# Branch a's operands, spilled rows and branch b's loads asked for at other steps

## The chip, the cores and the metric

The kernel runs on one core of one Trainium2 chip. The metric is the device time of one execution in microseconds. The kernel before took 1357.1 us, the median of 3 runs (1355.99 to 1358.39). Engines are named as in the profile: PE multiplies matrices, PEld loads its weights, DVE (vector), ACT (scalar) and POOL (GpSimd) work on tiles, SP issues most DMAs; POOL issues others on a queue of its own.

## The reference

One layer of an encoder on 1024 tokens of width 1024, in float32: a mixer of two branches merged by gates, then a SwiGLU network, each between two RMS norms. The mixer, cut to what the change touches:

```python
def mixer(h, w_in, b_f, conv_w, w_branch, w_out):
    proj = jnp.einsum("bsd,dn->bsn", h, w_in)
    q, k, v, f_logit, g_b, g_c, hc, gate_conv, gate_attn = jnp.split(proj, _SPLITS, axis=-1)
    ya = g_b * causal_depthwise_conv(g_c * hc, conv_w)
    ...
    yb = forgetting_attention(q.reshape(shp), k.reshape(shp), v.reshape(shp), logf)
    yb = yb.reshape(bsz, s_len, ATTN_WIDTH)
    ya_d = jnp.einsum("bsc,cd->bsd", ya, w_branch[0])
    yb_d = jnp.einsum("bsc,cd->bsd", yb, w_branch[1])
    merged = jax.nn.sigmoid(gate_conv) * ya_d + jax.nn.sigmoid(gate_attn) * yb_d
    return jnp.einsum("bsd,de->bse", merged, w_out)
```

Below, branch a is the convolution's (`ya`, `w_branch[0]`, `gate_conv`), branch b the attention's (`yb`, `w_branch[1]`, `gate_attn`).

## The kernel before, in words

Every float32 product is made of three matmuls on high and low halves (`split`, `mm3`): ACT copies the high half, DVE subtracts it for the low one. Most products use Strassen's scheme in Winograd's form: seven products of quarters (B11, B21, B22, T1 to T4 on the tokens' side; A11, A12, A22, S1 to S4 on the weights'). All instructions are recorded on line 76, so tile names tell them apart.

**Stages.** Up to 55 us the first norm and v; then the projections in 18 pairs of 128 columns (`jobs`, `strassen`, line 681; a pair is 84 matmuls on PE); from about 410 us attention in 21 steps (`steps`, line 1145; the loop adds two closing steps, t = 21 and 22), with branch a's products between them; from 551 us their end, from 588 branch b's eight 128-column products for each half of the tokens (`pbb`), then w_out, and the SwiGLU network from 632 us on.

**Side work of the projections.** Generators run a step at a time between the products of a pair (`plans`). `wa_steps` (line 762) makes branch a's weight operands: rows k and k+2 of `w_branch[0]` are loaded into `rows4`, four sums are formed there in two more quarters, everything is split and spilled to `wa_dram`; then `load_rows` (line 813) asks for the next pair of rows. The parts take turns in the tiles `r0`, `l0`, `h0`. `ya_steps` (line 819) does the same to the tokens of branch a, into `ya_ops`. A scheduler sets the order here, except for the instructions that are made while `strict` names their engine.

**Branch a within attention** (order written by hand: `strict[0] = engines`, line 1352). Its operands come back from memory. `load_y` (line 1363) loads a token operand (1 MB) into one of the four places h0, h1, l0, l1, by the table `HOME` (line 1360); `load_w` a weight operand (256 KB) into a ring of five small tiles (`s4`, two `s4h`, two `s4l`), in the order of use (`w_order`, `next_w`); `load_sg` a gate, in a ring of four. 28 chunks of six matmuls, P1 to P7 for each of four p (256 output columns each), are dealt to steps 2 to 22 (`chunks`, line 1510); the last six follow as `A_TAIL` (line 1519). P6 needs T1, P7 needs B22. A chunk's `drain` takes its PSUM bank into `um` on DVE, and P7 of a p goes into the bank of its P6. What is loaded at the end of step t stands in `at[t]` (lines 1569 to 1580). SP issues these DMAs one by one; one that waits holds up all behind it. In the same queue stand the reciprocals of the softmax sums (`inverse_rows`, line 1450): DVE copies `rT`, SP writes it (`ri_dram`), and reads it back as a broadcast (`rb`), twice at the end, for each half of the last head pair.

**Branch b.** `split_wb` splits its four blocks of weights (`raw`, then `wbh`, `wbl`) at steps 17, 19, 21, 22. In its loop (line 1791) the gate of each product is loaded, and in the first four passes a block of `w_out` (`load_wo`, line 1719); `strict` is empty there, so that the scheduler may issue them earlier.

## Time and profile before

| what | us |
|---|---|
| median of 3 runs | 1357.1 |
| profiled execution, its own time | 1352.99 |
| its span (first to last instruction) | 1351.2 |
| PE busy | 1309.4 |
| end of attention and branch a, 551 to 589: PE busy | 24.18 of 38 |
| branch b's products, 589 to 632: PE busy | 43.0 of 43 |
| projections, 300 to 396: PE busy | 78.8 of 96 |

In a row of the timeline come the start, the duration, the engine, line and operation, out<-in by the program's names, how many in a row, and in brackets how long the engine stood idle before it and what ended that. SPq rows are DMA issues; their duration is that of issuing.

### The profile page before, as it was taken

To read this page: it belongs to the slowest core of one execution; us is meant where nothing else is said; L and a number is where in the kernel's file an instruction comes from. 1 tells how busy PE (TensorE), PEld (TensorE's weight loads), DVE (VectorE), ACT (ScalarE), POOL (GpSimd) and SP (SyncE) were. 2 spreads that over 40 slices of the span, in tenths; PEclk is the share of its full clock that TensorE was granted. 3 is DMA by queue.
4 is the path that set the end of the run, shared out by engine and by line. 5 is a ranking of instruction groups with operands and counts; after the bars stand their busy time and mean duration, and the time that the engine had idled before them with its cause. 6 is when DMAs were issued, how large, how long until landed. Compare 5 with 4: busy or idle time off the path is not lost.

```text
span 1351.2 us, 17833 instructions
## 1 busy us (share of the span) xinstructions
PE 1309.4 (97%) x6671; PEld 1086.7 (80%) x6671; DVE 947.3 (70%) x1352; ACT 564.1 (42%) x875; POOL 210.6 (16%) x381
## 2 busy tenths in 40 slices
PE   9999999997889999789999999999999999999998
PEld 9988788886678888668888888888888888888886
DVE  7886778785565577667666779786666656676574
ACT  7533323343335666422567623322222323444451
POOL 3112111122222222000223212120111011000001
PEclk9999999998999999989999999999999999999999
DMA  6355545566765855586377655632333236966541
GB/s 227 100 166 179 188 140 172 171 210 239 253 225 183 277 181 191 193 278 221 110 190 245 203 164 181 193 133 86 117 101 117 87 116 226 362 243 198 162 164 63
DMA packets 184198, 245.08 MB, mean 181 GB/s; under 512 B 12440, under 2 KB 125152, under 8 KB 183216
## 3 DMA queue, kind: packets, MB, share of 16 engines
q1 hardware_dynamic: 158048, 156.07, 36.6%
q0 software_dynamic: 26048, 87.87, 17.6%
q8 instruction: 52, 0.85, 0.2%
q14 instruction: 34, 0.28, 0.1%
q10 hardware_dynamic: 16, 0.00, 0.0%
HBM read 168.09 MB, written 75.83 MB: 181 GB/s over the span
## 4 chain that ended last, share of the span: by engine, by line
PE 69%; DMA 2%; DVE 1%; issue 1%; SPq 0%; DVEq 0%; POOLq 0%; ACT 0%; POOL 0%; ACTq 0%
PE b L76 39%; PE pd L76 16%; PE pbb L76 3%; PE pba L76 3%; PE po L76 3%; PE tps L76 2%; PE sp L76 2%; PE ma L76 1%; PE mb L76 1%; PE tp L76 1%; DMA raw<-in_w_in_dram 0%; DMA s4l<-wa_dram 0%; DMA yT<-ya_ops 0%; DVE lo L76 0%; DMA ri_dram<-rT 0%
## 5 line engine op out<-in xcount | busy, mean ns | idle before, releaser
L76 DVE TENSOR_TENSOR c<-c,b 128x512 f32<-128x512 f32 x215 | 146.7, 683 | 71.1 <-PE b L76 69.5
L76 DVE TENSOR_TENSOR lo<-raw,hi 128x1024 fp32r<-128x1024 f32 (+1 forms) x91 | 109.6, 1205 | 66.0 <-PE b L76 49.5
L76 ACT ACTIVATE hi<-raw 128x1024 fp32r<-128x1024 f32 (+1 forms) x98 | 99.5, 1015 | 91.1 <-PE b L76 46.0
L76 ACT ACTIVATE hi<-sx 128x1024 fp32r<-128x1024 f32 x44 | 46.7, 1061 | 166.8 <-PE b L76 141.6
L76 DVE TENSOR_TENSOR sx<-raw 128x512 f32<-128x512 f32 x78 | 53.7, 689 | 58.1 <-DMA raw<-in_w_in_dram 26.9
L76 PE MATMUL b<-w12h,lo 128*128 128x512 f32 x208 | 80.9, 389 | 0.0
L76 PE MATMUL b<-w12h,hi 128*128 128x512 f32 x204 | 79.4, 389 | 0.0
L76 PE MATMUL b<-w12l,hi 128*128 128x512 f32 x204 | 79.4, 389 | 0.0
L76 DVE TENSOR_TENSOR lo<-sx,hi 128x1024 fp32r<-128x1024 f32 x44 | 53.8, 1223 | 33.9 <-PE b L76 29.2
L76 PE MATMUL b<-hh,hi 128*128 128x512 f32 x176 | 68.9, 392 | 0.0
L76 PE MATMUL b<-hl,hi 128*128 128x512 f32 x176 | 68.5, 389 | 0.0
L76 PE MATMUL b<-hh,lo 128*128 128x512 f32 x176 | 68.5, 389 | 0.0
L76 PE MATMUL b<-hT12h,lo 128*128 128x512 f32 x136 | 55.0, 405 | 12.1 <-DVE lo L76 12.0
L76 PE MATMUL b<-w,s4h 128*128 128x512 f32 x208 | 64.0, 389 | 0.0
L76 PE MATMUL pd<-hi,lo 128*128 128x512 f32 x160 | 62.3, 389 | 0.0
L76 PE MATMUL pd<-hi 128*128 128x512 f32 x160 | 61.9, 390 | 0.0
L76 POOL DMA_DIRECT2D a_dramA<-um x33 | 17.9, 543 | 276.7 <-DVE um L76 275.8
L76 PE MATMUL b<-hT34h,hi 128*128 128x512 f32 x136 | 53.3, 392 | 6.9 <-DVE c L76 6.9
L76 PE MATMUL pd<-ghi 128*128 128x512 f32 x148 | 57.6, 390 | 0.0
L76 PE MATMUL pd<-glo,ghi 128*128 128x512 f32 x148 | 57.6, 389 | 0.0
L76 PE MATMUL pd<-ghi,glo 128*128 128x512 f32 x148 | 57.6, 389 | 0.0
L76 PE MATMUL b<-hT12l,hi 128*128 128x512 f32 x136 | 54.1, 398 | 0.0
(478 smaller groups left out, 3608.4 us busy)
## 6 DMA issues: line engine op xcount, KB each, us to landing
raw<-in_w_gate_up_dram SPq DMA_DIRECT2D x52, 512.0 KB, 3.8
raw<-in_w_in_dram SPq DMA_DIRECT2D x35, 512.0 KB, 4.4
a_dramS<-um POOLq DMA_DIRECT2D x44, 256.0 KB, 2.9
a_dramA<-um POOLq DMA_DIRECT2D x33, 256.0 KB, 2.5
sg<-sg_dram SPq DMA_DIRECT2D x32, 256.0 KB, 2.9
graw<-a_dramS SPq DMA_DIRECT2D x14, 512.0 KB, 4.6
sg_dram<-c POOLq DMA_DIRECT2D x24, 256.0 KB, 2.7
raw<-in_w_down_dram SPq DMA_DIRECT2D x11, 512.0 KB, 5.6
```

What stands on the lines that cost most here:

```text
L76: ins = getattr(self.engine, name)(*args, **kw)
```

## The change

1. `wa_steps`: the two spills of the sums (`out(0, s)`, `out(2, u)`) come behind the splitting of the rows themselves, and the next rows are asked for between the two.
2. `ya_steps`: the next rows are asked for one step later.
3. `HOME`: B21 goes to h1 and T2 to l0. So T1 can follow B21 in h1 as soon as step 9 is done: it is loaded at step 10, not 19; T4 at 9, not 10. B22 is loaded at 19 as before, through POOL's queue.
4. Weights of branch a: three, not two, are asked for behind B21 ahead of the loop; the load of a step comes first in its list; a second one is asked for at steps 20 and 21 (before: 21 alone).
5. Branch b's weights: loaded at 13, 13, 16, 16 (before all at 16) and split at 16, 17, 21, 22.
6. The gates of branch b and the blocks of w_out are issued in a written order: two of each ahead of the loop, then one gate per pass, and a block in the first passes.

```diff
@@ wa_steps
-        out(0, s)
-        yield
-        out(2, u)
-        yield
         h, l = (half_tile(w0_tile(tags.popleft())) for _ in range(2))
...
             nc.gpsimd.dma_start(of(6, 1)(t), f32(h[:, t : t + 1]))
+        yield
+        out(0, s)
+        yield
         if k == 0:
             load_rows(wa_rows(1))
+        out(2, u)
         yield
@@ ya_steps
         out(4, b)
         out(6, a[:, :1])
+        yield
         if k == 0:
             load_rows(ya_rows(1))
-        yield
         out(0, t)
@@
-    HOME = dict(B11="h0", B21="l0", T2="h1", T3="l1", T4="h0", T1="h1", B22="l1")
+    HOME = dict(B11="h0", B21="h1", T2="l0", T3="l1", T4="h0", T1="h1", B22="l1")
...
-    def load_y(o):
+    def load_y(o, queue=nc.sync):
         yops[o] = yq.tile([P, 2, 2, NC], F32R, tag=f"y{HOME[o]}", name=f"y{o}", bufs=1)
-        nc.sync.dma_start(f32(yops[o]), ya_ops[SUMS_Y.index(o)])
+        queue.dma_start(f32(yops[o]), ya_ops[SUMS_Y.index(o)])
@@
-    for k, t in enumerate((17, 19, 21, 22)):
+    for k, t in enumerate((16, 17, 21, 22)):
         cuts[t].append(do(split_wb, k))
...
     for t in range(2, 23):
+        at[t].insert(0, next_w)
+    for t in (20, 21):
         at[t].append(next_w)
-    at[21].append(next_w)
-    for t, o in ((6, "T2"), (7, "T3"), (10, "T4"), (19, "T1"), (19, "B22")):
-        at[t].append(do(load_y, o))
+    for t, o in ((6, "T2"), (7, "T3"), (9, "T4"), (10, "T1")):
+        at[t].insert(0, do(load_y, o))
+    at[19].append(do(load_y, "B22", nc.gpsimd))
...
-    for k in range(4):
-        at[16].append(do(load_wb, k))
+    for k, t in enumerate((13, 13, 16, 16)):
+        at[t].append(do(load_wb, k))
@@
     load_y("B21")
-    for _ in range(2):
+    for _ in range(3):
         next_w()
@@
+    wo_raw = deque()
+
+    def next_wo():
+        if len(wo_raw) < 4:
+            wo_raw.append(load_wo(2 * len(wo_raw), n1))
@@
+    for _ in range(2):
+        next_wo()
+    bsg, bsg_order = [], deque((n, d) for n in range(2) for d in range(KT))
+
+    def next_bsg():
+        if bsg_order:
+            n, d = bsg_order.popleft()
+            bsg.append(sg_tile())
+            nc.sync.dma_start(bsg[-1], sg_dram[d][1, :, n * NC : (n + 1) * NC])
+
+    next_bsg()
+    next_bsg()
     divide(3, 1)
@@
-            sg = sg_tile()
-            nc.sync.dma_start(sg, sg_dram[d][1, :, ns])
+            sg = bsg[n * KT + d]
+            strict[0] = ("sync",)
+            next_bsg()
+            if n == 0:
+                next_wo()
+            strict[0] = ()
...
-                    load_wo(d * 2, n1),
+                    wo_raw[d],
```

What this does to the order shows best in the instruction lists. First SP's queue at the end of attention, steps 17 to 20, before. `ri_dram3` and `rb` are the round trip of the first half of the last reciprocals; `s4`, `s4h`, `s4l` from `wa_dram` are weights of branch a, `yT1` and `yB22` its last two token operands:

```order
L76 DMA raw_5553<-in_w_out_dram 128x2x512
L76 DMA ri_dram3_131<-rT_5205 4x128 x2
L76 DMA raw_5574<-in_w_out_dram 128x2x512
L76 DMA rb_5209<-ri_dram3_131 64x512 x2
L76 DMA s4_5245<-wa_dram_116 128x4x128
L76 DMA yT1_5247<-ya_ops_117 128x2048
L76 DMA yB22_5249<-ya_ops_117 128x2048
L76 DMA s4h_5318<-wa_dram_116 128x4x128
```

The same place now:

```order
L76 DMA s4_5162<-wa_dram_116 128x4x128
L76 DMA ri_dram3_131<-rT_5213 4x128 x2
L76 DMA rb_5217<-ri_dram3_131 64x512 x2
L76 DMA s4h_5249<-wa_dram_116 128x4x128
L76 DMA s4h_5320<-wa_dram_116 128x4x128
L76 DMA s4l_5322<-wa_dram_116 128x4x128
```

The weight of P6 p=0 (`s4`) has moved ahead of the round trip, the two token operands and the blocks of w_out are gone from here; two more weights (P6 p=1 and 2) follow that of P7 p=0 (`s4h`).

Second, SP's queue from step 21 into the tail, before; here `ri_dram3` and `rb` are the second half's round trip:

```order
L76 DMA s4l_5379<-wa_dram_116 128x4x128
L76 DMA sg_5381<-sg_dram2_137 128x512
L76 DMA raw_5595<-in_w_out_dram 128x2x512
L76 DMA ri_dram3_131<-rT_5396 4x128 x2
L76 DMA rb_5400<-ri_dram3_131 64x512 x2
L76 DMA s4l_5416<-wa_dram_116 128x4x128
L76 DMA sg_5418<-sg_dram5_140 128x512
L76 DMA s4_5439<-wa_dram_116 128x4x128
L76 DMA s4h_5452<-wa_dram_116 128x4x128
L76 DMA s4h_5465<-wa_dram_116 128x4x128
```

And now:

```order
L76 DMA s4l_5381<-wa_dram_116 128x4x128
L76 DMA s4_5383<-wa_dram_116 128x4x128
L76 DMA sg_5385<-sg_dram2_137 128x512
L76 DMA ri_dram3_131<-rT_5400 4x128 x2
L76 DMA rb_5404<-ri_dram3_131 64x512 x2
L76 DMA s4h_5420<-wa_dram_116 128x4x128
L76 DMA sg_5422<-sg_dram5_140 128x512
L76 DMA s4h_5443<-wa_dram_116 128x4x128
```

The weights of P6 p=3 (`s4l_5416` before, `s4l_5381` now) and of P7 p=1 (`s4_5439`, `s4_5383`) have moved ahead of the round trip; behind it stand those of P7 p=2 and 3 alone.

Third, ACT's order in the projections, at 121 to 130 us of the profile before. `rows4` holds rows of w_branch, `hi<-sx` is the high half of the next pair's weights. Before:

```order
L76 ACTIVATE hi_1419<-raw_1417 128x1024
L76 ACTIVATE c21_1456<-b1_1443 128x512
L76 ACTIVATE l0_1552<-rows4_970 128x512
L76 ACTIVATE hi_1429<-sx_1425 128x1024
L76 ACTIVATE so_1559<-b1_1443 128x512
```

Now:

```order
L76 ACTIVATE hi_1427<-raw_1425 128x1024
L76 ACTIVATE c21_1464<-b1_1451 128x512
L76 ACTIVATE r0_1482<-rows4_970 128x1024
L76 ACTIVATE l0_1554<-rows4_970 128x1024
L76 ACTIVATE h0_1703<-rows4_970 128x512
L76 ACTIVATE r0_1695<-rows4_970 128x512 x2
L76 ACTIVATE hi_1437<-sx_1433 128x1024
```

The copies of the first rows' sums (`r0_1482`, `l0_1554`) stand here now, and behind them the three copies of the second pair of rows (`h0_1703`, `r0_1695`), ahead of `hi<-sx`; before, those followed one pair later. On SP the second pair of rows is asked for two weight loads earlier than before, and on DVE its four sums still stand where they stood.

## The prediction

> **What bounds the kernel now.** I read the page first, then the matrix engine's waits, then that engine row by row where it waits, then the transfer queue behind those waits.

> The page's heading and busy line, and two rows of the table by stretches (us from the span's start, then busy us of PE, PEld, DVE, ACT, POOL, granted clock, DMA share, GB/s):

> ```profile
> span 1351.2 us, 17833 instructions
> PE 1309.4 (97%) x6671; PEld 1086.7 (80%) x6671; DVE 947.3 (70%) x1352; ACT 564.1 (42%) x875; POOL 210.6 (16%) x381
> ...
> 551.00:589.00 38.00, 24.18 (x130) 18.36 (x129) 20.74 (x36) 8.51 (x16) 2.30 (x3) 0.87 0.81 281
> 589.00:632.00 43.00, 43.00 (x191) 35.60 (x190) 34.51 (x50) 13.14 (x17) 4.03 (x6) 1.00 0.67 234
> ```

> PE is busy 97% of the span. Time can only go where PE stands idle, or works at half clock: 41.8 us in all. Of these, 13.8 lie in 551 to 589, where attention ends and branch a's last products run; the stage behind it has none. PE's waits, longest in total first:

> ```profile
> PE b L76 <- DVE lo L76: 12.0, 3, 6.4
> PE b L76 <- DVE c L76: 6.9, 3, 2.8
> PE pba L76 <- DMA s4l<-wa_dram: 6.5, 1, 6.5
> PE pba L76 <- DVE um L76: 3.5, 2, 2.0
> PE pba L76 <- DMA yT<-ya_ops: 2.8, 1, 2.8
> ```

> The two `b` waits belong to the projections before 410 us. The `pba` waits are branch a's, and two of them are transfers. PE there, row by row (start, duration, operation, in brackets the idle time before it):

> ```profile
> 555.13 1.66 PE L76 MATMUL pba<-yT,s4l 128*128 128x512 f32 x6 [1.50 <-DVE um L76]
> 559.54 2.49 PE L76 MATMUL pba<-yT,s 128*128 128x512 f32 x6 [2.75 <-DMA yT<-ya_ops]
> ...
> 565.95 0.74 PE L76 MATMUL tps<-ident,rows 128*128 128x128 f32 x5 [1.07 <-DVE um L76]
> ...
> 571.51 1.66 PE L76 MATMUL pba<-yT,s4h 128*128 128x512 f32 x6 [2.05 <-DVE um L76]
> 573.00 1.52 PE L76 MATMUL pba<-yT,s4l 128*128 128x512 f32 x6
> 580.98 2.93 PE L76 MATMUL pba<-yT,s4l 128*128 128x512 f32 x6 [6.45 <-DMA s4l<-wa_dram]
> ...
> 588.35 0.39 PE L76 MATMUL pbb<-yh,lo 128*128 128x512 f32 x1
> ```

> The waits add up: 1.50 + 2.75 + 1.07 + 2.05 + 6.45 = 13.8 us. In program order the chunks are P5 of p=3 (555.13), P6 of p=0 (559.54), P7 of p=0 (566.5), then P6 of p=1, 2, 3 and P7 of p=1, 2, 3. Why did the two loads come late? Their issues (SPq), and what stands around them:

> ```profile
> 552.09 1.12 SPq L76 DMA_DIRECT2D rb<-ri_dram  x2
> ...
> 553.91 0.62 SPq L76 DMA_DIRECT2D yT<-ya_ops  x1
> ...
> 570.59 0.27 DVE L76 COPY rT<-tr 8x128 f32<-8x128 f32 x1
> ...
> 570.88 0.60 SPq L76 DMA_DIRECT2D ri_dram<-rT  x2
> ...
> 574.21 1.12 SPq L76 DMA_DIRECT2D rb<-ri_dram  x2
> 575.43 0.68 SPq L76 DMA_DIRECT2D s4l<-wa_dram  x1
> ...
> 581.63 0.69 DVE L76 TENSOR_TENSOR um<-sg,um 128x512 f32<-128x512 f32 x1 [5.12 <-DMA sg<-sg_dram]
> ```

> T1 (1 MB, `yT`) is asked for at 553.91, 5.6 us before its product runs. The weights of P6 p=3 stand behind the round trip of the reciprocal rows (written at 570.88, read back from 574.21), so they are asked for at 575.43 and used 5.55 us later. That PE also ran at half clock shows in the stretches cut where the clock changes:

> ```profile
> 335.24:338.65 3.41, 1.10 (x5) 0.56 (x3) 3.41 (x4) 2.45 (x4) 1.35 (x3) 1.00 0.73 282
> ...
> 556.60:560.01 3.41, 0.66 (x3) 0.46 (x3) 0.00 (x0) 0.00 (x0) 0.00 (x0) 1.00 1.00 408
> 560.01:563.43 3.42, 3.42 (x19) 2.50 (x20) 0.00 (x0) 0.00 (x0) 0.00 (x0) 0.50 0.96 315
> ...
> 573.66:577.08 3.42, 0.86 (x4) 0.38 (x2) 2.81 (x5) 0.00 (x0) 0.46 (x1) 1.00 0.63 174
> 577.08:583.90 6.82, 2.92 (x7) 2.35 (x8) 0.69 (x1) 0.00 (x0) 0.75 (x1) 0.50 1.05 346
> ```

> A stretch of 3.41 us with PE busy 0.66 or 0.86 us was followed by half clock; one with 1.10 was not (339 on was fast). Work at half clock cost 3.42/2 = 1.7 us from 560.01, and 2.92/2 = 1.5 from 577.08.

> **The change, part by part.** 1. *T1 is asked for at step 10 instead of 19* (it takes the place of B21, done at step 9). Its wait of 2.75 goes: the load is 9 steps, some 50 us, early. What is late next is the PSUM bank of 555.13, which is there already. The half clock behind the wait goes too: 1.7. B22 goes to POOL's queue, idle there (its next DMA stood at 567.47), and is needed at 566.5; cost nothing. Together **4.4 us**.

> 2. *Weights one place further ahead.* Now the loads of P6 p=0 to 3 and P7 p=1 stand ahead of the second round trip, and P7 p=2 comes first behind it, in the very place where P6 p=3 stood. By the old clock it therefore lands at 580.98. PE gets there after the four chunks from 571.51 on at 1.49 us each (571.51 to 573.00) and two `pbb` matmuls of 0.23: 571.51 + 5.96 + 0.45 = 577.92. So 6.45 us of waiting become 580.98 − 577.92 = 3.06: **3.4 us**. P7 p=3 needs P6 p=3 drained, which DVE does behind the gate that waits for `sg` (581.63); gate and drain take 0.69 + 0.6, to 582.9; PE is there at 580.98 + 1.36 + 3 × 0.23 = 583.0. No new wait. The 1.5 us of half clock go if the stretches stay fast: **1.5 us**. Bounds: if the load lands no faster than the `s4l` and `sg` group of 557 to 566, some 8 us instead of 5.55, 2.5 us are lost; if PE drops to half clock once more, 1.7.

> [...]

> 3. *Weight splits of branch b at steps 16 and 17, not 17 and 19.* One DVE subtraction and one ACT copy more in step 16:

> ```profile
> 525.00:530.00 5.00, 5.00 (x58) 4.40 (x54) 3.67 (x13) 3.54 (x12) 1.72 (x4) 1.00 0.70 242
> 548.32 1.22 DVE L76 TENSOR_TENSOR wbl<-raw,hi 128x1024 fp32r<-128x1024 f32 x1
> ```

> DVE has 1.33 us spare in 5, the instruction takes 1.22: hidden, I take 0; without that cover at most 1.2. Step 19 gets it back, worth up to 0.3 at 555.13, also taken as 0.

> 4. *w_out and b's gates in written order* lie in 589 to 632, where PE never waits. The w_out loads now come behind the last gates of branch a, instead of up to 50 us early. DVE multiplies branch b's first products late anyway (594.74, PE began them at 588.35) and waits for PE from 618 on:

> ```profile
> 594.74 1.28 DVE L76 TENSOR_TENSOR sg<-sg,pbb 128x512 f32<-128x512 f32 x2
> ...
> 605.99 0.68 DVE L76 TENSOR_TENSOR sg<-sg,pbb 128x512 f32<-128x512 f32 x1
> ...
> 620.74 0.69 DVE L76 TENSOR_TENSOR sg<-sg,pbb 128x512 f32<-128x512 f32 x1 [1.31 <-PE pbb L76]
> ```

> Product 10 takes the bank that 605.99 empties, six products later, at about 588.35 + 10 × 2.72 − 0.45 = 615.1. Spare: 615.1 − 606.7 = 8.4 us. With PE 9 us earlier and DVE some 6, about 5 are left. Cost 0; without cover, what exceeds those 5.

> 5. *w_branch's operands in another order* (steps of `wa_steps`, 70 to 190 us). The piece of ACT's order above puts three copies, of the second pair of rows, ahead of `hi<-sx`. Before, that pair came late one projection pair further on, and PE paid for it:

> ```profile
> 155.78 0.50 PE L76 MATMUL b<-hT34h,hi 128*128 128x512 f32 x1 [1.71 <-DVE c L76]
> ...
> 152.83 1.04 ACT L76 ACTIVATE hi<-sx 128x1024 fp32r<-128x1024 f32 x1
> ...
> 128.91 1.07 ACT L76 ACTIVATE hi<-sx 128x1024 fp32r<-128x1024 f32 x1 [2.62 <-PE b L76]
> ...
> 671.41 19.07 PE b L76 x84
> ...
> 121.60 1.22 DVE L76 TENSOR_TENSOR rows<-rows,r 128x1024 fp32r<-128x1024 f32 x1
> ...
> rows<-in_w_branch_dram SPq DMA_DIRECT2D x2, 512.0 KB, 7.3
> ```

> From `hi<-sx` to PE's release are 155.78 − 152.83 = 2.95 us. Without the wait PE had gone on at 154.07, and one pair (84 matmuls, 19.07) earlier at 135.0: there `hi<-sx` may start until 132.05, and had 3.1 us spare. Now three subtractions of half the width stand where the one of 121.60 stood, and the rows are free behind them at about 123.5; asked for at 124 and landing in 7.3 they are there at 131.3; three copies of about 0.57 later, 133.0, PE has waited 0.95. So the 1.71 us turn into some 1 us, or into 0 if the rows come in 6 us, or 5 if they take 11 among the writes of `wa_dram`, which now share this time. I take no change; bounds −1.7 and +3.3.

> 6. *The row loads of branch a's tokens, one step later*: the order listing has every row of 200 to 410 us in its old place on every engine. 0, and the 17 us of `b` waits there stay.

> **Sum.** 4.4 + 3.4 + 1.5 = 9.3 us. The profiled execution took 1352.99 us, its span 1351.2 and 1.8 around it; that gives 1343.7. It was 4.1 us faster than the median of the runs, 1357.1, so the median becomes **1347.8**.

> **Rivals.** *The wait only moves.* P7 p=2 is still behind the round trip. If its load takes 8 us and the clock halves again, 9.3 − 2.5 − 1.7 = 5.1 are left: 1352.0. For it: this stretch already moves 281 GB/s at a DMA share of 0.81. Against: 2 MB of T1 and B22 and 1 MB of w_out leave it.

> *The early rows cost more.* ACT's copies wait 3 to 5 us for the second rows, and again one pair later: 1350 to 1353. **Slower** it becomes at one point: if the rows land more than 9.3 + 1.7 = 11 us after the 130.4 at which PE begins to wait (132.05 − 1.7 of copies), that is after 141.4, 17 us after their request; at 20 us it is 1360. The longest of such loads here took 7.3.

> *The change doesn't do it:* T1's wait is only covered by the bank's, or the tail's drains set the pace: about 1355.5, within 0.2%, which is about what a measurement of this kernel can tell from no change.

> **Chances.** Forecast (1345 to 1350) 0.60; the wait only moves 0.17; early rows, still faster, 0.11; no effect 0.08; slower 0.04. Faster by over 0.2% (below 1354.4): 0.88, same 0.08, slower 0.04. Range: 9.3 + 1.7 and 1 for the runs' spread give 1345 at the low end; the two dearer cases reach 1353. So 1344.8 to 1353.

> **What would show it.** Right: no wait of `pba` on `yT`, PE gap before P7 p=2 of about 3 us in place of 6.45 before P6 p=3, clock 1.00 through it, pbb begun about 9 us earlier, no idle PE behind it; in 120 to 160 us one wait of 1 us near 135 instead of 1.71 at 155.8. Wrong: a wait over 3 us near 135, idle PE among the `pbb`, or a second gap before P7 p=3.

## The result and the profile after

| | kernel before | changed kernel |
|---|---|---|
| first comparison, median (lowest to highest) | 1357.74 us, 4 runs (1355.99 to 1360.09) | 1346.01 us, 4 runs (1342.65 to 1347.01) |
| second, on another chip | 1355.83 us, 13 runs (1351.44 to 1358.27) | 1345.79 us, 5 runs (1342.19 to 1347.82) |
| profiled execution, its own time (span) | 1352.99 us (1351.2) | 1345.25 us (1343.5) |

The ratio of the changed kernel's time to the kernel before's is 0.9908 in the first comparison (95% interval 0.9884 to 0.9932) and 0.9923 in the second (0.9905 to 0.994). The medians fall by 11.7 and 10.0 us, the two profiled executions differ by 7.7 only: that of before happened to be a quick one, 4.8 us under its median.

Heading and busy line of the page after, then PE by stretches and PE's waits, columns as before:

```profile
span 1343.5 us, 17834 instructions
...
PE 1308.2 (97%) x6671; PEld 1086.1 (81%) x6671; DVE 947.5 (71%) x1352; ACT 564.5 (42%) x875; POOL 210.4 (16%) x382
```

```profile
551.00:589.00 38.00, 31.15 (x181) 24.73 (x178) 26.13 (x44) 13.83 (x24) 2.48 (x4) 0.96 0.77 259
589.00:632.00 43.00, 43.00 (x191) 35.59 (x190) 33.92 (x48) 9.55 (x11) 4.34 (x6) 1.00 0.81 283
```

```profile
PE b L76 <- DVE lo L76: 12.5, 3, 6.3
PE b L76 <- DVE c L76: 7.3, 3, 2.8
PE pba L76 <- DVE um L76: 3.2, 2, 2.0
PE pba L76 <- DMA s4h<-wa_dram: 2.5, 1, 2.5
```

The wait on `yT` is gone, and of the 6.5 us on weights 2.5 are left. PE's rows in the tail, from the timeline:

```profile
555.84 1.67 PE L76 MATMUL pba<-yT,s4l 128*128 128x512 f32 x6 [1.16 <-DVE um L76]
...
562.19 0.74 PE L76 MATMUL tps<-ident,rows 128*128 128x128 f32 x5 [1.14 <-DVE um L76]
...
567.75 2.25 PE L76 MATMUL pba<-yT,s4h 128*128 128x512 f32 x6 [2.05 <-DVE um L76]
...
575.39 1.52 PE L76 MATMUL pba<-yB,s4h 128*128 128x512 f32 x6
...
580.09 1.63 PE L76 MATMUL pba<-yB,s4h 128*128 128x512 f32 x6 [2.50 <-DMA s4h<-wa_dram]
```

Idle time adds up to 1.16 + 1.14 + 2.05 + 2.50 = 6.85 us where it was 13.8. The remaining wait is not where the prediction put it: P7 p=2 (575.39) does not wait, P7 p=3 (580.09) does. The transfers around it, POOL's issues, SP's, and the time from issue to landing of what is asked for between 570.5 and 573:

```profile
563.71 0.78 POOL L76 DMA_DIRECT2D w<-w_dram  x1 [14.08 <-ACT ptT L76]
571.17 0.77 POOL L76 DMA_DIRECT2D w<-w_dram  x1 [6.68 <-issue]
```

```profile
570.59 0.55 SPq L76 DMA_DIRECT2D s4h<-wa_dram  x1
...
571.90 0.55 SPq L76 DMA_DIRECT2D s4h<-wa_dram  x1
```

```profile
w<-w_dram POOLq DMA_DIRECT2D x1, 1024.0 KB, 8.3
s4h<-wa_dram SPq DMA_DIRECT2D x2, 256.0 KB, 3.4
```

The weights of P7 p=2 landed 3.4 us after their request. Those of P7 p=3, asked for 1.3 us later, were used 580.09 − 571.90 = 8.2 us after theirs. Between the two requests POOL had asked for a block of 1 MB (`w`, called w22 in the code, first used at 637.5 us). The gate that SP asks for between the two weights, at 571.20, was late as well: DVE waited for it until 576.73, 5.5 us after the request, before it could drain P6 p=3.

```profile
576.73 0.69 DVE L76 TENSOR_TENSOR um<-sg,um 128x512 f32<-128x512 f32 x1 [3.64 <-DMA sg<-sg_dram]
```

Half clock came back for one stretch. Windows of 3.41 us, cut where the clock changes:

```profile
336.47:339.88 3.41, 1.75 (x8) 1.43 (x9) 1.61 (x2) 1.58 (x2) 1.38 (x3) 1.00 0.86 279
339.88:343.30 3.42, 3.42 (x17) 2.82 (x16) 0.02 (x1) 0.00 (x0) 0.00 (x0) 1.00 0.99 234
...
565.16:568.57 3.41, 1.36 (x14) 0.99 (x11) 3.38 (x7) 2.67 (x5) 0.00 (x0) 1.00 0.90 285
568.57:571.99 3.42, 3.42 (x10) 2.64 (x9) 3.39 (x6) 0.00 (x0) 0.77 (x1) 0.50 0.34 97
```

568.57 to 571.99 ran at half clock: branch a's matmuls began 0.43 us apart there (10 in the window), 0.23 apart behind it. That is nearly twice, so I count half of the stretch as lost, 3.42/2 = 1.7 us, an estimate. It lies behind a window in which PE was busy 1.36 us; a window with 1.75 us had no such effect.

Last, w_branch's stage: ACT's rows, and PE's wait that follows from them:

```profile
121.70 1.06 ACT L76 ACTIVATE r<-rows 128x1024 fp32r<-128x1024 f32 x1 [0.52 <-DVE l L76]
130.00 1.06 ACT L76 ACTIVATE l<-rows 128x1024 fp32r<-128x1024 f32 x1 [7.23 <-DMA wa_dram<-l]
130.97 0.61 ACT L76 ACTIVATE h<-rows 128x512 fp32r<-128x512 f32 x1
131.96 1.15 ACT L76 ACTIVATE r<-rows 128x512 fp32r<-128x512 f32 x2 [0.38 <-issue]
133.02 1.04 ACT L76 ACTIVATE hi<-sx 128x1024 fp32r<-128x1024 f32 x1
```

```profile
135.97 0.50 PE L76 MATMUL b<-hT34h,hi 128*128 128x512 f32 x1 [1.82 <-DVE c L76]
```

One wait of 1.82 us at 136 stands where 1.71 at 155.8 stood. But ACT's 7.23 us of idle time end with a write, the spill of tile `l0` to `wa_dram` (asked for at 122.12, 7.9 us), and not with the rows: the first of the two, asked for at 121.10, had landed after 5.7 us, at 126.8.

### The profile page after: what moved, and what is told of

Its sections match the earlier page's. It is cut to its first block, busy times and chain, and to the rows that moved or that the text cites. A ratio compares the mean times of both kernels' runs of the same rounds, so it can differ in the third digit from the quotient of the medians.

```text
span 1343.5 us, 17834 instructions
## 1 busy us (share of the span) xinstructions
PE 1308.2 (97%) x6671; PEld 1086.1 (81%) x6671; DVE 947.5 (71%) x1352; ACT 564.5 (42%) x875; POOL 210.4 (16%) x382
## 4 chain that ended last, share of the span: by engine, by line
PE 72%; issue 18%; POOL 4%; DVE 2%; DMA 2%; ACT 1%; POOLq 0%; DVEq 0%; ACTq 0%; SPq 0%
PE b L76 40%; PE pd L76 16%; PE pbb L76 3%; PE pba L76 3%; PE tps L76 2%; PE po L76 2%; PE sp L76 2%; PE pv L76 1%; PE ma L76 1%; POOL sg_dram L76 1%; PE tp L76 1%; POOL ya_ops L76 1%; DVE lo L76 1%; DMA wa_dram<-r 1%; PE mb L76 1%
## 5 line engine op out<-in xcount | busy, mean ns | idle before, releaser
L76 DVE TENSOR_TENSOR c<-c,b 128x512 f32<-128x512 f32 x215 | 146.8, 683 | 74.2 <-PE b L76 71.4
L76 DVE TENSOR_TENSOR lo<-raw,hi 128x1024 fp32r<-128x1024 f32 (+1 forms) x91 | 109.6, 1205 | 70.5 <-PE b L76 53.1
L76 ACT ACTIVATE hi<-raw 128x1024 fp32r<-128x1024 f32 (+1 forms) x98 | 99.5, 1015 | 93.9 <-PE b L76 54.9
L76 ACT ACTIVATE hi<-sx 128x1024 fp32r<-128x1024 f32 x44 | 46.7, 1061 | 181.5 <-PE b L76 157.6
L76 DVE TENSOR_TENSOR sx<-raw 128x512 f32<-128x512 f32 x78 | 53.7, 689 | 51.8 <-issue 22.5
L76 DVE TENSOR_TENSOR lo<-sx,hi 128x1024 fp32r<-128x1024 f32 x44 | 53.8, 1223 | 38.8 <-PE b L76 31.2
L76 PE MATMUL b<-w12h,lo 128*128 128x512 f32 x208 | 80.9, 389 | 0.0
L76 PE MATMUL b<-w12h,hi 128*128 128x512 f32 x204 | 79.4, 389 | 0.0
L76 PE MATMUL b<-w12l,hi 128*128 128x512 f32 x204 | 79.4, 389 | 0.0
L76 PE MATMUL b<-hh,hi 128*128 128x512 f32 x176 | 69.0, 392 | 0.0
L76 PE MATMUL b<-hh,lo 128*128 128x512 f32 x176 | 68.5, 389 | 0.0
L76 PE MATMUL b<-hl,hi 128*128 128x512 f32 x176 | 68.5, 389 | 0.0
L76 PE MATMUL b<-hT12h,lo 128*128 128x512 f32 x136 | 55.0, 404 | 12.5 <-DVE lo L76 12.5
L76 PE MATMUL b<-w,s4h 128*128 128x512 f32 x208 | 64.1, 389 | 0.0
L76 PE MATMUL pd<-hi,lo 128*128 128x512 f32 x160 | 62.3, 389 | 0.0
L76 PE MATMUL pd<-hi 128*128 128x512 f32 x160 | 61.9, 390 | 0.0
L76 POOL DMA_DIRECT2D a_dramA<-um x33 | 17.9, 542 | 276.0 <-DVE um L76 275.4
L76 PE MATMUL b<-hT34h,hi 128*128 128x512 f32 x136 | 53.9, 396 | 7.3 <-DVE c L76 7.3
L76 PE MATMUL pd<-ghi 128*128 128x512 f32 x148 | 57.6, 390 | 0.0
L76 PE MATMUL pd<-glo,ghi 128*128 128x512 f32 x148 | 57.6, 389 | 0.0
L76 PE MATMUL pd<-ghi,glo 128*128 128x512 f32 x148 | 57.6, 389 | 0.0
L76 PE MATMUL b<-hT12l,hi 128*128 128x512 f32 x136 | 54.1, 398 | 0.0
## 6 DMA issues: line engine op xcount, KB each, us to landing
raw<-in_w_gate_up_dram SPq DMA_DIRECT2D x52, 512.0 KB, 3.9
raw<-in_w_in_dram SPq DMA_DIRECT2D x35, 512.0 KB, 4.3
graw<-a_dramS SPq DMA_DIRECT2D x14, 512.0 KB, 3.8
raw<-in_w_down_dram SPq DMA_DIRECT2D x11, 512.0 KB, 4.5
```

Source lines behind the costliest of these rows:

```text
L76: ins = getattr(self.engine, name)(*args, **kw)
```

## The experiments

Each kernel ran beside the kernel before on the same chip; the chips differ between some rows of the table, and before's median with them by up to 2 us, so rows are best compared by their ratios. "Idle" is the length of a stretch less PE's busy time in it, from the view by stretches of the run's one profiled execution, in us; the clock is the mean granted one from 545 to 590.

| run | median us (runs) | ratio to before, 95% | idle 60–200 | idle 300–410 | idle 545–590 | clock |
|---|---|---|---|---|---|---|
| before (the first profile) | 1357.74 (4) | 1 | 1.7 | 17.3 | 13.8 | 0.89 |
| changed (the first profile) | 1346.01 (4) | 0.9884–0.9932 | 1.8 | 17.9 | 6.9 | 0.96 |
| after_again | 1345.79 (5) | 0.9905–0.994 | 3.0 | 15.2 | 8.5 | 0.96 |
| tail_only | 1348.30 (6) | 0.9915–0.9954 | 1.5 | 14.6 | 7.6 | 0.92 |
| merge_only | 1356.01 (12) | 0.9985–1.0009 | 1.8 | 14.5 | 12.7 | 0.85 |
| old_wa | 1344.47 (5) | 0.9897–0.9928 | 2.6 | 14.6 | 6.3 | 0.96 |
| late_t1 | 1348.79 (6) | 0.9931–0.9965 | 1.9 | 15.7 | 10.3 | 0.96 |
| late_w | 1350.69 (8) | 0.9944–0.9975 | 2.9 | 16.3 | 8.9 | 0.89 |
| w22_late | 1348.23 (5) | 0.9927–0.996 | 1.8 | 14.5 | 6.7 | 1.00 |
| w22_sync | 1343.52 (6) | 0.9887–0.9923 | 1.8 | 16.2 | 7.0 | 0.96 |
| wa_mix0 | 1341.57 (4) | 0.9878–0.9919 | 1.3 | 14.3 | 5.9 | 0.96 |
| wa_mix | 1343.65 (5) | 0.9893–0.9926 | 2.0 | 13.6 | 6.2 | 0.96 |
| best | 1342.95 (5) | 0.9879–0.9916 | 1.2 | 12.4 | 6.5 | 1.00 |
| held | 1341.70 (5) | 0.9868–0.9908 | 2.2 | 14.8 | 4.3 | 1.00 |

**The changed kernel again** (after_again).

> The changed kernel itself once more, beside the others on one chip. Theory: 1346 plus or minus 1.5; waits in the tail within 0.5 us of the first profile's; the waits of the projections (300 to 410 us) differ by a microsecond or two from profile to profile, although nothing there was changed. Rival (those waits are the change's doing): 6.27 and 5.47 us again to a few tenths.

1345.79 us. The tail's small waits came out as in the first profile (1.16, 1.14, 2.06), but the one before P7 p=3 was 4.09 where it had been 2.50, which is outside the 0.5 us expected, and that near 136 was 3.03 where it had been 1.82. The waits of 300 to 410 us summed to 15.2, not 17.9. So a wait on a transfer, or behind one, moved by 1.6 and by 1.2 us between these two executions of one kernel, and I take a difference of that size between two single profiles to say nothing about an edit.

**The tail's parts alone** (tail_only): the kernel before with the changed kernel's `HOME`, `load_y`, places of the weights, `load_wb` and `split_wb`. The core of it:

```diff
-    for t, o in ((6, "T2"), (7, "T3"), (10, "T4"), (19, "T1"), (19, "B22")):
-        at[t].append(do(load_y, o))
+    for t, o in ((6, "T2"), (7, "T3"), (9, "T4"), (10, "T1")):
+        at[t].insert(0, do(load_y, o))
+    at[19].append(do(load_y, "B22", nc.gpsimd))
...
-    for _ in range(2):
+    for _ in range(3):
         next_w()
```

> The kernel before with only the parts on branch a's tail: T1, B22, the weights one place further ahead, branch b's weight loads and splits. The order of w_branch's pieces, of the token rows and the written order of w_out and branch b's gates are left as before. Theory (the earlier requests make the gain): no PE wait on T1, one wait of 2 to 4 us before P7 in place of 6.45 before P6 p=3, PE idle in the tail 7 us instead of 13.8, median 1346 to 1350, as the whole change. Rival (the gain comes from w_out's loads leaving the tail): the weights of P7 land in 5.5 us or more, PE waits 5 us or more before P7, and the median stays above 1351.

```profile
574.87 2.90 PE L76 MATMUL pba<-yB,s4h 128*128 128x512 f32 x6 [3.25 <-DMA s4h<-wa_dram]
```

No wait on T1, one of 3.25 us before P7 p=2, 7.6 us idle, 1348.3 us: the theory. Most of the gain is here; its interval overlaps the whole change's, so nothing is shown of the rest.

**The written order alone** (merge_only): the kernel before, with only `next_wo` and `next_bsg`.

```diff
-            sg = sg_tile()
-            nc.sync.dma_start(sg, sg_dram[d][1, :, ns])
+            sg = bsg[n * KT + d]
+            strict[0] = ("sync",)
+            next_bsg()
+            if n == 0:
+                next_wo()
```

> The kernel before with only the written order of w_out's loads and branch b's gates. Theory: PE's waits of 2.75 before P6 p=0 and 6.45 before P6 p=3 stay, time within 2 us of the kernel before. Rival (w_out's loads crowd the tail): the 6.45 shrink by 2 to 3 us, and the time falls by 3 to 5 us.

```profile
557.86 2.36 PE L76 MATMUL pba<-yT,s 128*128 128x512 f32 x6 [3.41 <-DMA yT<-ya_ops]
...
576.66 2.93 PE L76 MATMUL pba<-yT,s4l 128*128 128x512 f32 x6 [3.79 <-DMA s4l<-wa_dram]
```

The time is that of before, 0.9997 of it. The wait on the weights is shorter in this profile (3.79), as the rival had it, but T1's is longer (3.41), and by the run of the changed kernel again such sizes are not settled by one profile. The time decides: no effect (the lower end of its interval, 0.9985, is a gain of 2.0 us, short of the rival's 3 to 5).

**T1 late again** (late_t1).

```diff
-    for t, o in ((6, "T2"), (7, "T3"), (9, "T4"), (10, "T1")):
+    for t, o in ((6, "T2"), (7, "T3"), (9, "T4")):
         at[t].insert(0, do(load_y, o))
-    at[19].append(do(load_y, "B22", nc.gpsimd))
+    at[19].append(do(load_y, "T1"))
+    at[19].append(do(load_y, "B22"))
```

> The changed kernel with T1 asked for at step 19 again, B22 on SP's queue behind it. Theory: a wait of some 2.75 us before P6 p=0 on T1, half clock after it for 1.7 more: 4.4 us slower than the changed kernel, 1350.4. Rival (the wait was only covered by the PSUM bank's, or the weights' wait behind it absorbs it): 0 to 1 us slower.

```profile
559.20 1.67 PE L76 MATMUL pba<-yT,s 128*128 128x512 f32 x6 [2.88 <-DMA yT<-ya_ops]
```

The wait is back, a tenth of a microsecond over its old size. The median is 1348.79 − 1345.9 = 2.9 us higher (1345.9 lies between the two medians of the changed kernel), but on another chip; the ratios differ by 0.0025 and 0.0040, which is 3.4 and 5.4 us, each with an interval of some 2.3 us to either side. So the time doesn't tell the wait alone from the wait with the half clock that the theory added. The profile does: none followed this wait, which the grid of the clock cut in two, with 1.67 and 1.98 us of work in the two windows. The tail's half clock came behind the wait of 2.55 us before P7 p=3.

**The weights late again** (late_w).

```diff
     for t in range(2, 23):
-        at[t].insert(0, next_w)
-    for t in (20, 21):
         at[t].append(next_w)
+    at[21].append(next_w)
...
-    for _ in range(3):
+    for _ in range(2):
         next_w()
```

> The changed kernel with the weights asked for in their old places (two at the start, then one at the end of each step). Theory: a wait of 5 to 6.5 us before P6 p=3 comes back, and with it half clock behind it (1.5), 3.4 + 1.5 = 4.9 us slower than the changed kernel, 1351. Rival (the changed kernel's wait before P7 is as good as any other): no more than 2 us slower.

```profile
578.28 2.90 PE L76 MATMUL pba<-yT,s4l 128*128 128x512 f32 x6 [3.35 <-DMA s4l<-wa_dram]
...
583.25 2.04 PE L76 MATMUL pba<-yB,s 128*128 128x512 f32 x4 [1.22 <-DMA s<-wa_dram]
```

The time is as expected, 1350.7, 4.9 us up from after_again on the same chip, and the two intervals lie apart. Its parts are not as expected: PE waits 3.35 and 1.22 us on weights, hardly more in all than in after_again (4.09). More of it is half clock, granted 0.89 in this stretch where after_again has 0.96: the work done at half clock, 8.32 us against 2.99, cost an estimated 8.32/2 = 4.2 us against 2.99/2 = 1.5. The profiled execution was the slowest of the eight (1354.43), so these parts need not be those of the median.

**The second half of w_branch's steps.** First the old order as a whole (old_wa):

> The changed kernel with w_branch's pieces in the old order. Theory: the wait of 1.8 us near 136 goes, one of 1.7 us near 155.8 comes back, median 1346 plus or minus 1.5. Rival (the new order was worth something, or cost something): 1348 and more, or 1344 and less.

1344.47 us, between the theory's range (from 1344.5) and the rival's (to 1344): the wait of 1.72 us at 156.6 came back, the one at 136 went, and by the ratios (0.9912 against 0.9908 and 0.9923) the time stayed. Then the old order for the first half and the new one for the second (wa_mix0), and the same with the tiles in turn, which the first two lines of the diff add (wa_mix):

```diff
-        tags = deque(("r0", "l0", "h0") * 2)
+        tags = deque((("r0", "l0", "h0") * 4)[5 * k : 5 * k + 5])
...
+        if k == 0:
+            out(0, s)
+            yield
+            out(2, u)
+            yield
         h, l = (half_tile(w0_tile(tags.popleft())) for _ in range(2))
```

> The changed kernel with w_branch's first half in the old order and the second half in the new one. Theory (ACT's copies wait until the spills of the tiles that they write have landed): no wait near 136; near 150 ACT begins its copies of the second rows only when r0's spill has landed (asked near 141.4, 8.8 us), hi<-sx starts near 152, PE waits about 0.9 us near 155. Rival (the rows' landing decides): the copies begin near 146.5, hi<-sx starts by 150.5, PE doesn't wait. Time within 1.5 us of the changed kernel either way.

> As the run with w_branch's halves in different orders, and in the second half the three tiles in turn (h0, r0, l0 where it was r0, l0, h0), so that the first copies write a tile whose spill is long done. Theory (ACT waits for spills): the first copy of the second rows begins with their landing near 146.5, not near 149.4, and only the last half-width copy waits for a spill, that of l0 near 150.5; hi<-sx at 151.1 to 151.5, PE waits at most 0.4 us near 155. Rival (the copies wait for DVE's sums or the rows): they begin near 149.4 again. Time within 1 us of that run.

ACT in wa_mix0, then in wa_mix:

```profile
149.40 1.15 ACT L76 ACTIVATE r<-rows 128x512 fp32r<-128x512 f32 x2 [8.39 <-DVE rows L76]
```

```profile
146.12 0.63 ACT L76 ACTIVATE h<-rows 128x512 fp32r<-128x512 f32 x1 [5.33 <-DMA rows<-in_w_branch_dram]
148.96 0.63 ACT L76 ACTIVATE h<-rows 128x512 fp32r<-128x512 f32 x1 [2.21 <-DMA rows<-in_w_branch_dram]
151.00 0.63 ACT L76 ACTIVATE l<-rows 128x512 fp32r<-128x512 f32 x1 [1.41 <-DVE rows L76]
```

wa_mix0 by itself does not decide. DVE had the first rows at 146.58, ACT began at 149.40; the spill of `r0`, asked for at 141.27, took 8.0 us and landed just before, at 149.2, but the profile names DVE as the releaser. PE waited 0.22 us at 154.2, where the theory had 0.9 and the rival nothing. wa_mix decides: with a tile whose spill was long done, ACT's first copy began with the landing of the rows (146.12). So in wa_mix0 a spill of the tile to be written held ACT for some 3 us (149.40 against 146.12 in wa_mix), as theory had it. The gain at PE failed to come. ACT's last copy, into `l0`, began at 151.00, just after that tile's spill had landed (asked for at 141.95, 8.9 us; the profile names DVE), `hi<-sx` at 151.54 (wa_mix0: 150.98), and PE waited 0.82 us at 154.6, twice the 0.4 allowed, and 0.81 at 184.2 (idle 60–200 still 2.0). The times missed too: 1341.57 us is 4.2 under after_again on the same chip, where 1.5 was allowed, and 1343.65 is 2.1 over wa_mix0, a kernel meant to be alike, where 1 was. All three intervals overlap, so nothing is won or lost that these runs can tell.

**Who makes the last weights late?** First w22 behind w12 on POOL's queue (w22_late), by a written order there; then, in the second diff, w22 on SP's queue among branch b's gates (w22_sync):

```diff
+    strict[0] = ("gpsimd",)
     load_sum([t[:, 1] for t in w12], 1, 1)
     load_sum([t[:, 0] for t in w12], 0, 0)
     for t, o in enumerate(w22):
         nc.gpsimd.dma_start(f32(o), w22_dram[t].rearrange("k p c -> p k c"))
+    strict[0] = ()
```

```diff
-    for t, o in enumerate(w22):
-        nc.gpsimd.dma_start(f32(o), w22_dram[t].rearrange("k p c -> p k c"))
...
+            if (n, d) in ((0, 5), (1, 1)):
+                nc.sync.dma_start(f32(w22[n]), w22_dram[n].rearrange("k p c -> p k c"))
             strict[0] = ()
```

> The changed kernel with POOL's two loads of w22 (1 MB each, needed from 650 us on) behind those of w12, so that they leave the stretch of 564 to 580. Theory (the last weights land late because they share this stretch with w22): they land in 3.5 to 4.5 us in place of 8.2, the wait of 2.5 us before P7 p=3 shrinks to 0.5 or less, P7's drains come some 2 us earlier, 2 to 3 us faster than the changed kernel, 1343 to 1344. Rival (the drain of P6 p=3 behind its gate sets P7 p=3): the wait stays at 2 us and changes only its releaser to DVE, time within 0.7 us.

> The changed kernel with the two loads of w22 on SP's queue, among branch b's gates (behind its products 5 and 9), instead of on POOL's queue at 564 and 571. Theory (the last weights of P7 land late beside w22): PE idle before P7 is 1.5 to 2.4 us in all, as with w22 behind w12, and the wait of 7.2 us on w3 near 638 is gone: 1.5 to 2.5 us faster than the changed kernel, about 1344. Rival (the loads only move the crowding): a wait of over 1 us among branch b's products or in the first products of w_out, time no better than the changed kernel's.

PE and POOL in w22_late:

```profile
572.38 1.62 PE L76 MATMUL pba<-yB,s4h 128*128 128x512 f32 x6 [1.47 <-DMA s4h<-wa_dram]
...
575.58 1.65 PE L76 MATMUL pba<-yB,s4h 128*128 128x512 f32 x6 [0.88 <-DVE um L76]
...
638.57 0.79 PE L76 MATMUL b<-wl,raw 128*128 128x512 f32 x1 [7.17 <-DMA wl<-wt_dram]
```

```profile
566.62 0.79 POOL L76 DMA_DIRECT2D w12h<-wt_dram  x1 [20.02 <-DVE yl L76]
...
585.00 0.77 POOL L76 DMA_DIRECT2D w12l<-wt_dram  x1 [17.59 <-DVE yl L76]
...
631.10 0.76 POOL L76 DMA_DIRECT2D wl<-wt_dram  x1 [7.16 <-issue]
```

The median is 2.4 us over the changed kernel's on the same chip, with intervals that overlap, and not 2 to 3 under it: a miss. POOL's nine loads of 1 MB went one after the other here, from 585.00 on asked for 5.9 to 9.1 us apart, w3's (`wl`, `wh`) last in both orders. With w12 first, the second load (`w12l`) waited for DVE's `yl` until 585.00; POOL stood still from some 574, when the first had landed (7.7 us), in a time in which it moves w22 in the changed kernel. So w3's last two blocks were asked for at 631.10 and 638.83 (616.92 and 624.51 in the changed kernel), and PE stood 7.17 us at 638. And the tail got less than hoped for: with w22 out of the way, POOL started its next load, `w12h`, at 566.62, and now P7 p=2 waited.

In w22_sync the wait at 638 is gone, but `w12h` again goes out beside the weights of P7 p=2, which take 6.9 us, and PE waits longer than the 1.5 to 2.4 us expected:

```profile
578.17 2.90 PE L76 MATMUL pba<-yB,s4h 128*128 128x512 f32 x6 [2.69 <-DMA s4h<-wa_dram]
```

Its 1343.52 us are the theory's 1344, but at a ratio of 0.9905 it is not told apart from the changed kernel, nor from the rival's "no better". So one edit more keeps POOL quiet there (held; "best" is the same without it: wa_mix and w22_sync together):

```diff
+    strict[0] = ("gpsimd",)
+    nc.gpsimd.tensor_scalar(st_tile("va"), um[:, 7, 0:1], EPS, None, op0=ALU.add)
     load_sum([t[:, 1] for t in w12], 1, 1)
     load_sum([t[:, 0] for t in w12], 0, 0)
+    strict[0] = ()
```

> Both together: w_branch's halves in different orders with the tiles in turn, and w22 on SP's queue among branch b's gates. Theory: the two gains add up, 1.5 to 2 us from w_branch and 1.5 to 2.5 us from the tail, 1342 to 1343; rival: no better than the changed kernel with w_branch's halves in different orders.

> The combination of before with one more edit: POOL's first load of w12 waits for the last of branch a's gates (a one-column operation on POOL that reads that gate's output stands ahead of it), so no 1 MB load of POOL lies between 560 and 580 us. Theory (whichever 1 MB load POOL starts beside the last weights makes them late, and taking one away only let the next one start): both weights land 3 to 4 us after their requests, PE waits 0 on the weights before P7, and at most 1.5 us on DVE's drain of P6; about 1 us faster than the combination. Rival (these weights are slow of themselves, or because of the gates' loads on their own queue): they land after 5 us or more, and PE waits 0.8 us or more on them as in the combination.

POOL's issues in held, how long the first weights took, DVE's wait for the gate, and PE by stretches:

```profile
579.77 0.59 POOL L76 TENSOR_SCALAR va<-um 128x1 f32<-128x1 f32 x1 [31.28 <-DVE um L76]
580.72 0.84 POOL L76 DMA_DIRECT2D w12h<-wt_dram  x1 [0.36 <-ACT yh L76]
```

```profile
s4h<-wa_dram SPq DMA_DIRECT2D x1, 256.0 KB, 3.5
```

```profile
572.61 0.69 DVE L76 TENSOR_TENSOR um<-sg,um 128x512 f32<-128x512 f32 x1 [0.99 <-DMA sg<-sg_dram]
```

```profile
564.76:568.17 3.41, 1.55 (x7) 1.29 (x8) 3.38 (x6) 2.62 (x5) 0.00 (x0) 1.00 0.01 1
568.17:571.59 3.42, 3.42 (x17) 2.84 (x16) 3.39 (x6) 0.00 (x0) 0.00 (x0) 1.00 0.64 216
545.00:590.00 45.00, 40.66 (x255) 33.28 (x254) 36.70 (x61) 18.66 (x31) 3.20 (x5) 1.00 0.64 214
```

With POOL quiet, P7 waits neither for weights nor for a drain, and 4.3 us of idle time are left in the tail. The gate came 3.6 us after its request (569.04), not 5.5. That matters, for in five profiles with a 1 MB load in this place (old_wa, wa_mix0, wa_mix, best, w22_late) the wait before P7 p=3, 0.9 to 2.0 us, ended with DVE's drain of P6 p=3 behind that gate and not with the weights, as the rival of w22_late had it. In old_wa the gate took 7.1 us (569.00 to 576.09), and:

```profile
577.43 1.66 PE L76 MATMUL pba<-yB,s4h 128*128 128x512 f32 x6 [1.95 <-DVE um L76]
```

So two transfers set the start of P7 p=3, its weights and the gate of its bank, and both came later with a large load beside them: the gate after 5.5 us in the changed kernel and 7.1 in old_wa, where held has 3.6; the weights after 8.2 in the changed kernel, while in held PE didn't wait for them.

The combination took 1342.95 us, inside the theory's 1342 to 1343, but that two gains added up is not shown: it is 0.7 under wa_mix on the same chip and 1.4 over wa_mix0, which is the rival's outcome. The kernel held took 1341.70 (ratio 0.9888, 0.9868 to 0.9908): the shortest waits of the tail, and four of its five runs lie below the quickest of the changed kernel's nine (1342.19). Its interval still overlaps the changed kernel's, and the step from the combination, 1.25 us, is within the spread of the runs.

## Why the prediction was right, and where its steps failed

The forecast of 1347.8 us was 1.8 above the median, inside its range, and the main reasons hold: late_t1 and late_w each bring a wait and time back, tail_only alone gives most of the gain. Two of the prediction's own signs of being wrong showed all the same: a gap before P7 p=3 (2.50 and 4.09), and in after_again a wait over 3 us near 135 (3.03 at 138). Point by point:

1. **T1 at step 10: right, but for the half clock.** late_t1 gives the wait back (2.88, forecast 2.75) and 2.9 us by the medians. The 1.7 us of half clock behind it don't come with T1's wait as a rule: they came in the profile before and in merge_only, not in late_t1.

2. **Weights one place ahead: the size right, the place wrong.** Forecast 3.06 us before P7 p=2 and "no new wait" before P7 p=3; measured 0 and 2.50 (4.09 in the second profile). The failed step is "by the old clock it therefore lands at 580.98": the weights of P7 p=2 landed in 3.4 us, not 5.55, and the next ones took 8.2. For P7 p=3 the sum asked only after DVE's drain, never after its weights. I had followed SP's queue and left out what POOL moved at the same time: before, the late weights had been asked for 2.08 us behind a w22 block, now those of P7 p=2 go 0.58 us ahead of it and those of p=3 0.73 behind. In w22_late and w22_sync another 1 MB load, `w12h`, stood beside the weights of P7 p=2, and PE waited 1.47 and 2.69 us for them; in held, with no such load, they landed after 3.5 us and PE didn't wait. So I put the lateness down to a 1 MB load of POOL's beside them, whichever it is.

**Half clock: the stretch with 1.10 us was misread.** I took it that 1.10 us of work in a window save the clock. That stretch, 335.24 to 338.65, lay across two windows. On the grid on which the clock changes the rows before are:

```profile
334.73:338.14 3.41, 1.61 (x8) 0.99 (x6) 3.41 (x4) 2.45 (x4) 1.63 (x3) 1.00 0.58 228
338.14:341.56 3.42, 2.82 (x12) 2.32 (x13) 0.55 (x1) 1.33 (x2) 1.09 (x2) 1.00 0.91 235
```

So 1.61 saved it, and 1.36 (after, 565.16) did not. The stretch behind the wait of 2.05 us, which nobody had touched, halved the clock in place of the two that went: of the forecast 3.2 us of half clock 1.5 were gained. In after_again it was the stretch behind the wait of 4.09 us instead.

3. **Splits at 16 and 17: the 0.3 us named as possible.** The wait at 555.13 went from 1.50 to 1.16; it is 1.50 in merge_only and 1.16 in all twelve profiles that have the new splits.

4. **The written order: nothing, as forecast.** merge_only is at 0.9997 of before, and PE is busy 43.0 of 43 us behind the tail.

5. **w_branch's steps: the balance right, the mechanism wrong.** One wait for another, and old_wa runs as fast. But what held ACT were spills of tiles about to be written again (ACT's 7.23 us ended with `wa_dram<-l`), not the landing of the second rows; wa_mix moved ACT's first copy to the landing by a change of tiles alone. That `hi<-sx` began at 133.02, as forecast (133.0), is luck: the rows came 4.5 us earlier than forecast (126.8, not 131.3), and the spill made up for it.

6. **The token rows one step later: not tried alone.** PE is busy 100.0 of 100 us from 200 to 300 in all fourteen profiles.

**The sum.** Two landmarks bound the part from attention to the first product of w_out, here after the change:

```profile
411.44 0.39 PE L76 MATMUL ma<-hB11h,hi 128*128 128x512 f32 x1
...
623.94 0.39 PE L76 MATMUL b<-w11h,raw 128*128 128x512 f32 x1
```

They stood at 409.90 and 631.42 before. So this part took 221.5 us and takes 212.5: 9.0 us gained, 9.3 forecast. Idle time in the tail gave 13.82 − 6.85 = 7.0 (forecast 6.1) and half clock 1.5 (forecast 3.2); the last 0.5 I did not trace. That the totals agree to 0.3 us is partly luck, since the errors cancel; with after_again's wait of 4.09 the idle time would have given 1.6 less. The part ahead of it took 1.5 us longer in this execution. No edit lies between 200 and 410 but the moved row load, and idle time from 300 to 410 goes from 12.4 to 17.9 us over the fourteen profiles, so I read it as chance, not as a price of the change. It makes up 1.5 of the 4.0 us by which the profiles differ less than the medians; the rest I did not trace.

## What to carry to other kernels

When a load is asked for earlier, look for the next late one right behind it: here a wait of 6.45 us before P6 p=3 went, and one of 2.50 before P7 p=3 came. Look at what every queue moves in those microseconds, not only at the queue that is waited for: beside a large load, not needed for another 66 us, the last small one came 8.2 us after its request, where the one ahead of it had taken 3.4. Moving that load only let the next one start in its place (`w12h`, at 566.62 in w22_late), until POOL was made to wait for an event behind the tail (580.72 in held). And before a copy is put ahead of others on an engine, ask when the tile that it writes has been spilled, not only when its input lands: here ACT stood until 130.00 behind a spill, with its rows landed at 126.8.

## What the runs showed of the hardware

Transfers. How long 256 KB of weights on SP's queue took beside a 1 MB load of POOL's went with which of the two was asked for first, down to tenths of a microsecond. Beside a block of w22, weights asked for 0.13 to 0.63 us ahead of it landed, or were used, after 3.0 to 4.0 us (eight profiles; 3.4 in the changed kernel). Those asked for 0.19 to 0.93 us behind it, where PE waited for them, were used after 7.1 to 8.3 (tail_only, changed, after_again, late_t1, late_w), and those 2.08 us behind it, in the kernel before, after 5.55. Ahead of another load, `w12h`, by 0.06 or 0.07 us they took 5.0 to 6.9 (best, w22_late, w22_sync). With none beside them it was 3.5 (held). No run changed the order of the two requests alone, so that the order is the cause is read from these profiles, not tested.
